# A third seven-product job in the input of a gated short convolution, and another order of the jobs around it

## The chip, the cores and the metric

The kernel runs on one core of a Trainium2 chip. The engines are TensorE (PE, with its weight loads PEld), VectorE (DVE), ScalarE (ACT), GpSimd (POOL) and SyncE (SP), which only issues DMAs. The metric is device microseconds of one execution, the median of three runs.

## The reference

The model has two layers on 512 tokens of width 1024, batch 1, float32: a gated short convolution with a SwiGLU, then sliding-window attention with a SwiGLU. The change lies in the first mixer alone:

```python
def short_conv_mixer(h, w_in, conv_w, w_out):
    bcx = h @ w_in
    b_gate, c_gate, u = jnp.split(bcx, 3, axis=-1)
    y = b_gate * causal_depthwise_conv3(c_gate * u, conv_w)
    return y @ w_out
```

Its input is rmsnorm(x) with a gain, its output is normed and added to x. Each of b, c and u is a product of 512 x 1024 by 1024 x 1024.

## The kernel before

**Numbers in two parts.** Every float32 matrix that enters a matmul is split into a high part (`whi`, a copy by ScalarE, in `split_weights` and `Job.prepare`, L500) and a low part (`wlo`, a subtraction on VectorE, L501). A product is three matmuls, `mm3`, L208 to L210. The channels of b, c and u are cut in eight tiles of 128, numbered f = 0 to 7; a tile's product over eight blocks of the inner dimension is a *project* of 24 matmuls of 512 columns (`pcub` in the rows).

**Seven products.** For c and u of two neighbouring tiles the kernel forms a 2 x 2 block product with seven block products in place of eight (`cross_jobs`, L908): four raw blocks a11, a12, a21, a22 of weights, sums of them made by VectorE (`make_two`, `make_three`, `make_four`, L917), sums of the tokens made once for all (`SUMMED`), and seven jobs of 24 matmuls of 256 columns. They collect in three PSUM banks, X for the products 1, 6, 7, 4, Y for 2, Z for 5 and 3 (`gx`, `gy`, `gz`). `take` reads the banks out between: products 1, 6 by ScalarE into `st`, 5 by ScalarE into `u`, 2, 3, 7 by a VectorE addition, 4 by two VectorE products which give c times u for both tiles in `gr`. Product 4 goes on adding in bank X, so its first matmul may start only when the take of product 7 (L949, `st<-gx`) has read it. Behind product 4 come, tile by tile: the product with the row norms (L854), a scaled copy by ScalarE and two taps by VectorE (L863), the product with b (L869). Tiles 2 and 3 then make a pair for the output product (sums and splits, L613 to L624); tiles 4 to 7 are split alone into `yhi` and `ylo` (L873, L874).

**Before the change** this form serves tiles 2, 3 (jobs X1 to X7) and 4, 5 (Y1 to Y7). b of these tiles is a project (b2 to b5, `gate_job`) which ScalarE copies from PSUM to SBUF (`bry`, L904). Tiles 6 and 7 have three projects each (c6 u6 b6, c7 u7 b7, `conv_jobs`), and the product with b reads PSUM. The output product of tiles 0 to 3 is again seven jobs P1 to P7 of 12 matmuls of 512 columns (`px`, `py`, `pz`), whose results go to `mix` by ScalarE's copies (L670) or VectorE's additions (L672). The weights of the other half, w0 to w3, are jobs that prepare and run nothing.

**What sets the order.** The string `CONV` lists the jobs by hand, and `in_line` (L505) runs them: run job j, prepare the weights of job j + 3 (`LINE_LEAD`), fetch raw blocks as buffers come free (`N_RAW` = 7 raw, `N_W` = 4 split ones), then one deferred step of an earlier job. Each of the engines PE, DVE, ACT and POOL keeps that order. `begin` and `pace` start sums of later weights by GpSimd's DMAs behind some jobs. Behind the line comes `close`: the output product of tiles 4 to 7 with w0 to w3 (`pmix`), in whose first part the weights of the feed-forward (gu, L438 and L443) are split, and which reads the parts of tile 7 last.

## Time and profile before

| | before |
|---|---|
| median of 3 runs | 1009.86 us (1009.26 to 1010.09) |
| the profiled execution | 1009.68 us |
| its span, first to last instruction | 1007.8 us |
| granted TensorE clock, mean | 0.999 |
| PE, DVE, ACT, POOL busy | 999.5, 911.1, 609.3, 184.3 us |
| DMA | 246.61 MB, mean 245 GB/s |

A row of a timeline has the start and the length in us, engine, line, operation, output and inputs by the program's names, the shape, the count of instructions merged in the row, and, in brackets, idle time before it with what ended it. Starts on an engine lie closer than the lengths, since an instruction begins while the one before drains; a step's price in a full queue is the distance of starts. The ends of matmuls are modelled. The rows of the trace carry the line numbers of the kernel before.

### The profile page before, as it was taken

What the parts mean: (1) busy time and instruction counts of PE and PEld (TensorE: products, weight loads), DVE (VectorE), ACT (ScalarE), POOL (GpSimd) and SP (SyncE); (2) the same over time, 40 slices, a digit from 0 to 9 for tenths busy, and PEclk for the clock granted to TensorE, in tenths of its full rate; (3) what the DMA queues carried; (4) which work ended last, traced back from release to release, by engine and by line L of the source; (5) the groups of instructions that cost most, each with busy time, mean ns of one, the idle gap of its engine ahead of it and who ended that gap; (6) DMA issues with size and microseconds to landing.
All of it is one profiled execution on the core that took longest, in us unless ns stands there. A gap on an engine that the chain in (4) does not pass through costs nothing.

```text
span 1007.8 us, 16460 instructions
## 1 busy us (share of the span) xinstructions
PE 999.5 (99%) x6008; PEld 886.7 (88%) x6008; DVE 911.1 (90%) x1564; ACT 609.3 (60%) x1105; POOL 184.3 (18%) x250
## 2 busy tenths in 40 slices
PE   9999999999999999999999999999999999999997
PEld 8899888999889898998898888799998988989986
DVE  7898878899799999999888998988997999999996
ACT  7445545875655455566485788777666564545641
POOL 0211021212111011000122756321201010110001
PEclk9999999999999999999999999999999999999999
DMA  9895988669979699779504889967989587979742
GB/s 338 263 260 181 334 283 288 204 194 286 343 243 297 220 303 321 236 219 336 193 1 138 216 245 245 292 242 170 305 285 319 167 251 237 289 272 276 243 167 83
DMA packets 67873, 246.61 MB, mean 245 GB/s; under 512 B 8017, under 2 KB 8657, under 8 KB 56017
## 3 DMA queue, kind: packets, MB, share of 16 engines
q1 hardware_dynamic: 52624, 148.07, 39.4%
q0 software_dynamic: 14592, 96.48, 37.7%
q8 instruction: 47, 0.77, 0.3%
q10 hardware_dynamic: 576, 1.02, 0.3%
q14 instruction: 34, 0.27, 0.1%
HBM read 239.25 MB, written 102.76 MB: 339 GB/s over the span
## 4 chain that ended last, share of the span: by engine, by line
PE 97%; DVE 2%; ACT 1%; issue 0%; DVEq 0%
PE gx L1282 15%; PE gx L1285 8%; PE px L208 4%; PE px L209 4%; PE px L210 4%; PE pmix L210 3%; PE pmix L208 3%; PE pmix L209 3%; PE gz L1282 3%; PE pcub L208 2%; PE pcub L210 2%; PE pcub L209 2%; PE gy L209 2%; PE gy L208 2%; PE gy L210 2%; PE pz L210 2%
## 5 line engine op out<-in xcount | busy, mean ns | idle before, releaser
L501 DVE TENSOR_TENSOR wlo<-raw,whi 128x1024 fp32r<-128x1024 f32 (+1 forms) x231 | 279.0, 1212 | 25.7 <-ACT whi L500 25.6
L500 ACT ACTIVATE whi<-raw 128x1024 fp32r<-128x1024 f32 (+1 forms) x231 | 239.7, 1051 | 79.2 <-DVE raw L488 37.7
L1282 PE MATMUL gx<-xt,whi 128*128 128x512 f32 x480 | 120.6, 393 | 0.0
L1282 PEld LDWEIGHTS gx<-xt,whi 128*128 128x128 f32 x480 | 86.2, 189 | 15.7
L571 POOL DMA_DIRECT2D hsum<-in_w_gb_dram x96 | 63.6, 727 | 163.0 <-ACT whi L500 107.8
L571 POOL DMA_DIRECT2D hsum<-hsum x32 | 25.2, 788 | 351.3 <-ACT whi L500 248.9
L1260 ACT ACTIVATE st<-gx 128x256 f32<-128x256 f32 x120 | 43.4, 380 | 60.9 <-PE gx L1285 57.3
L1237 DVE TENSOR_TENSOR st<-gx,st 128x256 f32<-128x256 f32 x200 | 77.4, 417 | 2.2 <-ACT st L1260 0.4
L1285 PEld LDWEIGHTS gx<-xt,wlo 128*128 128x128 f32 x480 | 65.5, 190 | 4.7
L1285 PE MATMUL gx<-xt,wlo 128*128 128x256 f32 x480 | 66.9, 282 | 0.0
L1296 ACT ACTIVATE gr<-gr 128x1024 f32<-128x1024 f32 x20 | 21.2, 1062 | 55.7 <-DVE gr L1237 55.7
L208 PE MATMUL gy<-xlo,whi 128*128 128x256 f32 x176 | 49.8, 283 | 0.0
L209 PE MATMUL gy<-xhi,whi 128*128 128x256 f32 x176 | 49.8, 283 | 0.0
L210 PE MATMUL gy<-xhi,wlo 128*128 128x256 f32 x176 | 49.8, 283 | 0.0
L208 PE MATMUL px<-wlo,ahi 128*128 128x512 f32 x120 | 46.7, 389 | 0.0
L209 PE MATMUL px<-whi,ahi 128*128 128x512 f32 x120 | 46.7, 389 | 0.0
L210 PE MATMUL px<-whi,alo 128*128 128x512 f32 x120 | 46.7, 389 | 0.0
L571 POOL DMA_DIRECT2D hsum<-in_w_dn_dram x48 | 32.0, 762 | 69.3 <-ACT whi L500 47.4
L1282 PE MATMUL gx<-xhl,whi 128*128 128x512 f32 x160 | 39.9, 391 | 0.0
L672 DVE TENSOR_TENSOR mix<-mix,px 128x512 f32<-128x512 f32 x54 | 34.8, 680 | 2.1 <-PE px L210 2.1
L318 POOL TENSOR_TENSOR ur<-uv,mhalf 128x1 f32<-128x1 f32 x15 | 13.9, 927 | 113.0 <-DVE uv L313 112.9
L488 DVE TENSOR_TENSOR raw<-raw,raw 128x1024 f32<-128x1024 f32 x28 | 34.1, 1218 | 0.1
(359 smaller groups left out, 3052.3 us busy)
## 6 DMA issues: line engine op xcount, KB each, us to landing
hsum<-in_w_gb_dram POOLq DMA_DIRECT2D x96, 512.0 KB, 8.0
raw<-hsum SPq DMA_DIRECT2D x88, 512.0 KB, 7.9
raw<-in_w_gb_dram SPq DMA_DIRECT2D x60, 512.0 KB, 6.9
hsum<-in_w_dn_dram POOLq DMA_DIRECT2D x36, 512.0 KB, 8.1
raw<-in_w_dn_dram SPq DMA_DIRECT2D x32, 512.0 KB, 7.0
hsum<-hsum POOLq DMA_DIRECT2D x28, 512.0 KB, 5.5
hsum<-in_w_dn_dram POOLq DMA_DIRECT2D x12, 768.0 KB, 13.5
raw<-in_w_in_dram SPq DMA_DIRECT2D x13, 512.0 KB, 7.2
```

The costliest lines, as they stand in the source:

```text
L208: nc.tensor.matmul(out, whi, xlo, start=start, stop=False, **kw)
L209: nc.tensor.matmul(out, whi, xhi, start=False, stop=False, **kw)
L210: nc.tensor.matmul(out, wlo, xhi, start=False, stop=stop, **kw)
L488: nc.vector.tensor_tensor(out=raw, in0=raw, in1=self.raws[1].tile, op=ALU.add)
L500: self.begun = nc.scalar.activation(hi[:, :n], raw, AF.Copy)
L501: nc.vector.tensor_tensor(out=lo[:, :n], in0=raw, in1=hi[:, :n].bitcast(F32), op=ALU.subtract)
L571: nc.gpsimd.dma_start(dst, src, max_dma_last_dim=4 * 4 * S, **kw))
L672: nc.vector.tensor_tensor(out=m, in0=m, in1=banks[bs][r], op=ALU.subtract if half else ALU.add)
L1237: nc.vector.tensor_tensor(out=out, in0=a, in1=b, op=ALU.add)
L1260: nc.scalar.activation(ste, a, AF.Copy)
L1282: nc.tensor.matmul(banks[c][e], whi[:, kk], factors[p][k][2], start=opened and k == 0, stop=False, **kw)
L1285: nc.tensor.matmul(banks[c][e][:, :256], wlo[:, kk], factors[p][k][0], start=False, stop=k == 3 and p in (4, 5), **kw)
```

## The change

`CROSS` goes from (2, 6) to (2, 8): c and u of tiles 6 and 7 become a third job of seven block products, Z1 to Z7, and c6, u6, c7, u7 go, with the function `conv_jobs`. The gates are spread: b4 stays between X and Y, b5 moves from behind Y6 to behind Y4, b6 stands between P6 and P3, b7 behind P4, w0 and w1. Where a tile's other factor is done before its gate (`later_on`: tiles 5, 6, 7), the product with b reads PSUM and ScalarE's copy falls away. The loads of x for the closing update (`hs`) are issued at the end of Z instead of Y. Their starts of sums move with the gates.

```diff
 CONV = (
-    "b2 b3 X1 X2 X6 X5 X7 X3 X4 b4 Y1 Y2 Y6 b5 Y5 Y7 Y3 Y4 c6 P1 P5 P6 P3 u6 P7 P2 P4 b6 w0 c7 u7 w1 b7 w2 w3"
+    "b2 b3 X1 X2 X6 X5 X7 X3 X4 b4 Y1 Y2 Y6 Y5 Y7 Y3 Y4 b5 Z1 Z2 Z6 Z5 Z7 Z3 Z4 "
+    "P1 P5 P6 b6 P3 P7 P2 P4 w0 w1 b7 w2 w3"
 )
-CROSS = (2, 6)
+CROSS = (2, 8)
...
-    BEGUN = {"X": {3: "c3"}, "Y": {6: "c4", 3: "c5"}}
+    BEGUN = {"X": {3: "c3"}, "Y": {6: "c4", 3: "c5"}, "Z": {}}
+    later_on = {}
     def gate_job(f, pool):
+        banks = []
         def products(job):
             ps = bank("pcub", pool)
+            banks.append(ps)
             project(ps, job.w, xs)
-            brs[f] = slot("bry")
-            nc.scalar.activation(brs[f], ps, AF.Copy)
-        return Job([Raw(w_in[f, 2])], products, begin("c2") if f == 3 else None)
+            if f not in later_on:
+                brs[f] = slot("bry")
+                nc.scalar.activation(brs[f], ps, AF.Copy)
+        def then():
+            parts = []
+            if f in later_on:
+                third, end = later_on[f]
+                parts = [lambda: third(banks[0])] + end()
+            if f in (3, 6, 7):
+                begin(f"c{f if f > 3 else 2}")()
+            if f < KT - 1:
+                return parts
+            for part in parts:
+                part()
+        return Job([Raw(w_in[f, 2])], products, then)
...
         def end():
-            steps = [conv(f + e, kept[2], brs.pop(f + e)) for e in range(2)]
-            parts = [lambda: [s[0]() for s in steps], steps[0][1], steps[1][1],
-                     lambda: [s[2](None) for s in steps]]
-            for s in steps:
-                parts += s[3]()
-            if f + 2 == CROSS[1]:
-                for b in range(NB):
-                    hs[b] = wide("h")
-                    tc.keep_in_program_order(nc.sync.dma_start(hs[b], x[b]))
+            steps = [conv(f + e, kept[2], brs.get(f + e)) for e in range(2)]
+            parts = [lambda: [s[0]() for s in steps], steps[0][1], steps[1][1]]
+            for e in range(2):
+                if f + e in brs:
+                    parts.append(lambda e=e: steps[e][2](None))
+                    parts += steps[e][3]()
+                else:
+                    later_on[f + e] = steps[e][2:]
+            if f < KT - 2:
+                return parts
+            for b in range(NB):
+                hs[b] = wide("h")
+                tc.keep_in_program_order(nc.sync.dma_start(hs[b], x[b]))
             return parts
-    def conv_jobs(f, pools):
...
-    for f, pool in zip(range(*CROSS), "ppmm"):
+    for f, pool in zip(range(*CROSS), "ppmmmm"):
         line[f"b{f}"] = gate_job(f, pools[pool])
-    for f, c in zip(range(*CROSS, 2), "XY"):
+    for f, c in zip(range(*CROSS, 2), "XYZ"):
         line.update(cross_jobs(f, c))
```

The order of instructions moves as follows; a number at a name is that of the buffer, and the lines of the kernel after stand one or some twenty higher.

VectorE in the Y block, from the sums of the pair of tiles 2 and 3 (`s`, `alo`) to the take of product 7 (`st<-gx`). Before, `wlo_1103` is Y3's low part and `wlo_1147` Y4's:

```order
L501 TENSOR_TENSOR wlo_1103<-raw_776,whi_1102 128x1024
L617 TENSOR_TENSOR s_929<-yy_926 128x256
L618 SCALAR_TENSOR_TENSOR s_929<-s_928,yy_926 128x256
L624 TENSOR_TENSOR alo_1117<-s_928,ahi_1116 128x512
L501 TENSOR_TENSOR wlo_1147<-raw_781,whi_1146 128x1024
L624 TENSOR_TENSOR alo_1155<-s_929,ahi_1154 128x512
L624 TENSOR_TENSOR alo_1159<-yy_926,ahi_1158 128x512
L949 TENSOR_TENSOR st_968<-gx_970,st_968 128x512
```

The same place after, with `wlo_1062` for Y3, `wlo_1109` for Y4 and `wlo_1146` for b5:

```order
L936 TENSOR_TENSOR raw_776<-raw_776,raw_579 128x1024
L870 TENSOR_TENSOR yy_926<-t_927,bry_666 128x512
L502 TENSOR_TENSOR wlo_1062<-raw_776,whi_1061 128x1024
L615 TENSOR_TENSOR a_231_930<-yy_926,a_231_930 128x256
L618 TENSOR_TENSOR s_928<-yy_926 128x256
L619 SCALAR_TENSOR_TENSOR s_928<-s_928,yy_926 128x256
L502 TENSOR_TENSOR wlo_1109<-raw_781,whi_1108 128x1024
L618 TENSOR_TENSOR s_929<-yy_926 128x256
L619 SCALAR_TENSOR_TENSOR s_929<-s_928,yy_926 128x256
L625 TENSOR_TENSOR alo_1117<-s_928,ahi_1116 128x512
L968 TENSOR_TENSOR st_968<-gx_970,st_968 128x512
L502 TENSOR_TENSOR wlo_1146<-raw_819,whi_1145 128x1024
```

The second product with b (`yy<-t,bry`) now stands between the sum of blocks and Y3's split, and the take stands two `alo` earlier. On TensorE the 24 matmuls of b5 no longer lie between Y6 and Y5.

ScalarE behind P4, whose bank goes to `mix` in two copies. Before, `raw_1427` is c7's block and `raw_1429` u7's:

```order
L192 ACTIVATE whi_1478<-raw_1191 128x512
L192 ACTIVATE whi_1479<-raw_1191 128x512
L670 ACTIVATE mix_1342<-px_1303 128x512
L670 ACTIVATE mix_1344<-px_1304 128x512
L500 ACTIVATE whi_1500<-raw_1427 128x1024
L500 ACTIVATE whi_1529<-raw_1429 128x1024
```

After, `raw_1630` is b7's block, and `raw_1632` and `raw_1760` are those of w2 and of the first gu:

```order
L193 ACTIVATE whi_1679<-raw_1399 128x512
L193 ACTIVATE whi_1680<-raw_1399 128x512
L276 DMA G_1687<-in_behind_dram 128x1024
L671 ACTIVATE mix_1546<-px_1508 128x512
L671 ACTIVATE mix_1548<-px_1509 128x512
L501 ACTIVATE whi_1704<-raw_1630 128x1024
L193 ACTIVATE whi_1708<-raw_1632 128x512
L439 ACTIVATE whi_1777<-raw_1760 128x1024
```

The two copies are followed by b7's high part where c7's stood, and the load of G comes ahead of them.

TensorE at the same place, after: the last matmuls of P4 and the first of b7 (before, the 24 of b6 follow P4):

```order
L209 MATMUL px_1509<-wlo_1627,ahi_1155 128x512
L210 MATMUL px_1509<-whi_1626,ahi_1155 128x512
L211 MATMUL px_1509<-whi_1626,alo_1156 128x512
L209 MATMUL pcub_1724<-xhl_221,whi_1704 128x512
L210 MATMUL pcub_1724<-xhl_221,whi_1704 128x512
L211 MATMUL pcub_1724<-xhl_221,wlo_1705 128x512
```

b7's first matmul stands right behind P4's last, and its third reads the low part.

More of the change, by code (lines that the diff above doesn't have):

```diff
@@ L1049, in yoco_kernel @@
     pools = {"p": ps_pt, "m": ps_mm, "s": ps_sc}
-    for f, pool in zip(range(*CROSS), "ppmm"):
+    for f, pool in zip(range(*CROSS), "ppmmmm"):
         line[f"b{f}"] = gate_job(f, pools[pool])
-    for f, c in zip(range(*CROSS, 2), "XY"):
+    for f, c in zip(range(*CROSS, 2), "XYZ"):
         line.update(cross_jobs(f, c))
-    for f, of in zip(range(CROSS[1], KT), ("mms", "spm")):
-        for c, job in zip("cub", conv_jobs(f, [pools[p] for p in of])):
-            line[f"{c}{f}"] = job
     for n in range(4):
```

28 lines of the change are left out of this document (removed).

## The prediction

> **What bounds the kernel now.** I read the page first (busy times and the chain that ended last), then who waits on TensorE over the whole span, then the window of the convolution input, then the order of time on TensorE, VectorE (DVE) and ScalarE (ACT) at the places that the change touches. The head of the page and of its chain:
>
> ```profile
> span 1007.8 us, 16460 instructions
> ...
> PE 999.5 (99%) x6008; PEld 886.7 (88%) x6008; DVE 911.1 (90%) x1564; ACT 609.3 (60%) x1105; POOL 184.3 (18%) x250
> ...
> PE 97%; DVE 2%; ACT 1%; issue 0%; DVEq 0%
> ```
>
> The waits of TensorE in the whole span (engine and line, whom it waited for, total us, times, longest), and the window that holds the stage (busy us and count of PE, PEld, DVE, ACT, POOL, then the granted clock, DMA share, GB/s):
>
> ```profile
> PE idle L748 <- DVE ones L152: 1.1, 1, 1.1
> PE pt L1603 <- DVE plo L1620: 0.4, 1, 0.4
> ```
>
> ```profile
> 46.00:153.00 107.00, 107.00 (x632) 95.47 (x631) 94.00 (x119) 52.65 (x74) 14.91 (x22) 1.00 0.85 262
> ```
>
> TensorE waits 1.5 us in all, and nowhere in this stage: it is the bound, and each microsecond of wait that the change makes lengthens the kernel, as each one of matmuls that it saves shortens it. VectorE comes second: 94.0 of 107.0 us, 13 us free.
>
> **What a matmul costs here.** Starts on TensorE, in order: first matmul of X4, of Y1, of b5 (behind Y1, Y2, Y6), of b6, and of the closing stage (behind b6, c7, u7, b7):
>
> ```profile
> 67.00 0.28 PE L208 MATMUL gx<-xf,whi 128*128 128x256 f32 x1
> ...
> 75.34 0.28 PE L208 MATMUL gx<-xhl,whi 128*128 128x256 f32 x1
> ...
> 83.98 0.40 PE L208 MATMUL pcub<-xhl,whi 128*128 128x512 f32 x1
> ...
> 130.90 0.39 PE L208 MATMUL pcub<-xhl,whi 128*128 128x512 f32 x1
> ...
> 152.66 0.39 PE L208 MATMUL pmix<-wlo,yhi 128*128 128x512 f32 x1
> ```
>
> Three jobs of 24 matmuls of 256 columns take 83.98 - 75.34 = 8.64 us, so 0.120 each and 2.88 a job. Four of 24 of 512 columns take 152.66 - 130.90 = 21.76, so 0.2267 each and 5.44 a job. The change takes c6, u6, c7, u7 out (96 matmuls, 21.76 us) and puts Z1 to Z7 in (7 x 2.88 = 20.16): **-1.60 us**, the whole of the gain, and under 0.2% (2.02 us), which is about what a measurement of this kernel tells from no change.
>
> [...] The rows above show 120 and 227, and the sum goes by them.
>
> **VectorE and ScalarE.** These rows of VectorE (start, length) price its steps by the distance from start to start. First those of the X block, then the beginning of the Y block:
>
> ```profile
> 56.53 0.68 DVE L869 TENSOR_TENSOR yy<-cut,pcub 128x512 f32<-128x512 f32 x1
> ...
> 57.73 1.22 DVE L501 TENSOR_TENSOR wlo<-raw,whi 128x1024 fp32r<-128x1024 f32 x1
> 58.86 1.22 DVE L917 TENSOR_TENSOR raw<-raw,raw 128x1024 f32<-128x1024 f32 x1
> 59.99 0.42 DVE L614 TENSOR_TENSOR a<-yy,a 128x256 fp32r<-128x256 f32 x1
> ...
> 61.21 1.23 DVE L501 TENSOR_TENSOR wlo<-raw,whi 128x1024 fp32r<-128x1024 f32 x1
> 62.35 0.42 DVE L617 TENSOR_TENSOR s<-yy 128x256 f32<-128x256 f32 x1
> ...
> 63.02 0.68 DVE L624 TENSOR_TENSOR alo<-s,ahi 128x512 fp32r<-128x512 f32 x1
> 63.62 1.22 DVE L501 TENSOR_TENSOR wlo<-raw,whi 128x1024 fp32r<-128x1024 f32 x1
> ...
> 65.96 0.68 DVE L949 TENSOR_TENSOR st<-gx,st 128x512 f32<-128x512 f32 x1
> ...
> 77.12 1.23 DVE L501 TENSOR_TENSOR wlo<-raw,whi 128x1024 fp32r<-128x1024 f32 x1 [1.75 <-ACT whi L500]
> 78.26 1.29 DVE L854 TENSOR_TENSOR gr<-gr,rrow 128x512 f32<-128x512 f32 x2
> ...
> 81.19 1.22 DVE L501 TENSOR_TENSOR wlo<-raw,whi 128x1024 fp32r<-128x1024 f32 x1
> 82.33 1.53 DVE L863 SCALAR_TENSOR_TENSOR t<-gr,gt,t 128x511 f32<-128x511 f32 x2
> 83.78 0.68 DVE L945 TENSOR_TENSOR gr<-gy,st 128x512 f32<-128x512 f32 x1
> ```
>
> A split of weights or a sum of blocks takes 1.13, a step on 512 columns 0.60, a pair of taps 1.45. The change adds three splits, four sums and five takes (3.4 + 4.5 + 3.0) and drops two products with u and two first taps (about 2.2): 8.7 us more, on VectorE, in 1.6 us less. Of 13 us free some 3 remain: enough in the mean, so what counts is where work piles up. ScalarE gets three splits more and loses copies; at 52.65 of 107 us its load costs nothing, its order does (below). DMA traffic stays the same, four blocks for four tiles of weights. The products with b read PSUM instead of a copy: as the first row above (yy<-cut,pcub, 0.68) shows, at the price of a product from SBUF. b5's bank is held some 17 us longer; its pool has four, and the next to want it is b6, 11 us after it is free.
>
> **Place 1: Y4.** In both orders the take of product 7 (st<-gx) reads the X bank that product 4 adds to, so Y4's first matmul waits for it. In the X block, where no gate stands between the seven, the take ended at 65.96 + 0.68 = 66.64 and X4 began at 67.00: 0.36 us to spare. Before, b5 stood in the Y block and gave VectorE 5.44 us more; now it comes behind Y4. Up to 82.33 nothing on VectorE moves (the row at 81.19 was b5's split and is now Y5's). From there its order is: taps to 83.78, third product and take of Y2 1.20 to 84.98, split of Y7 to 86.11, sum of blocks to 87.24 and third product to 87.84. Y3's split must wait for ScalarE, which can begin only when the sum has ended (86.11 + 1.22 = 87.33) and takes as long as here:
>
> ```profile
> 60.11 1.06 ACT L500 ACTIVATE whi<-raw 128x1024 fp32r<-128x1024 f32 x1 [0.91 <-DVE raw L917]
> ```
>
> So Y3's split runs from 88.45 to 89.59; three sums of the pair (59.99 to 61.21, 1.22) to 90.81; split of Y4 1.14 to 91.95; two sums 0.67 to 92.62; alo 0.60 to 93.22; the take ends 0.68 later, at 93.90. TensorE comes to Y4 at 75.34 + 6 x 2.88 = 92.62. **+1.3 us**; without the wait for ScalarE (0.6) and the pair's gap it would be 0.6, with a second wait of that size 1.9.
>
> **Place 2: Z4**, the same shape without pair sums. With Y4 from 93.92, TensorE comes to Z4 at 93.92 + 2.88 + 5.44 + 17.28 = 119.52. VectorE from 93.82: split of b5, two alo, take 3, split of Z1, sum, two takes, split of Z2, two sums (1.14 + 1.2 + 0.6 + 1.13 + 1.13 + 1.2 + 1.13 + 2.27 = 9.8) to 103.6; a wait of 1.2 for ScalarE's part of Z6; split, two products with the row norms, split of Z5, four taps, take 2, split of Z7, sum, third product (1.14 + 1.2 + 1.14 + 2.9 + 0.6 + 1.14 + 1.13 + 0.6 = 9.85) to 114.7; a wait of 0.6 for ScalarE's part of Z3; then split, ylo, split of Z4 with 0.2 of wait, third product of b5 and the take (1.14 + 0.6 + 0.2 + 1.13 + 0.6 + 0.68) to about 119.65. **+0.15 us**, between 0 and 0.5.
>
> **Place 3: b7.** A job's weights are split right behind the run of the job three places ahead in the line. Before, P4 was followed by b6 w0 c7: c7's split stood behind P4, and b6 ran meanwhile. Now it is P4 w0 w1 b7, and w0 and w1 run nothing on TensorE: b7's split stands behind P4 with no matmul between. On ScalarE it is queued behind the two copies of P4's bank, which wait for P4's last matmuls, and w2's and the next stage's splits queue behind it. c7's place in the trace:
>
> ```profile
> 130.42 1.28 ACT L670 ACTIVATE mix<-px 128x512 f32<-128x512 f32 x2 [4.55 <-PE px L210]
> 131.60 2.00 ACT L500 ACTIVATE whi<-raw 128x1024 fp32r<-128x1024 f32 x2
> ```
>
> P4 ended where b6 began, at 130.90, so the split starts 0.70 behind P4, its high part is ready at 0.70 + 1.05 = 1.75, VectorE's low part 1.22 + 0.03 later at 3.00, and with it the third matmul, the first that reads it. Without a wait that one starts at 2 x 0.2267 = 0.45. 2.55, and a little for TensorE to start again: **+2.6 us**, between 2.4 and 3.1 (before, VectorE came to that split 0.4 late). b7's raw block is no limit: by VectorE's steps the buffer that b6's split frees is its own, some 17 us ahead.
>
> **The end of the stage** I cost at nothing: y7's parts stand behind the splits of four weights of the feed-forward (gu), as before, when they ended 0.3 us ahead of the matmul that reads them:
>
> ```profile
> 154.05 0.68 DVE L869 TENSOR_TENSOR bry<-cut,pcub 128x512 f32<-128x512 f32 x1
> ...
> 155.78 0.68 DVE L874 TENSOR_TENSOR ylo<-bry,yhi 128x512 fp32r<-128x512 f32 x1
> ```
>
> The four loads of h move behind w1's on SyncE's queue, to about 119 us by VectorE's steps, and are first read in the closing stage's update.
>
> **Sum** on the profiled execution (1009.68, its span 1007.8 and 1.9 around it; 0.18 under the median of 1009.86): -1.60 + 1.3 + 0.15 + 2.6 = +2.45, so 1012.1, and by the median **1012.3 us**.
>
> **Rivals.**
>
> *VectorE keeps up* (not slower by the bound). Places 1 and 2 cost nothing, if the take of Y7 ends by 92.62, that is if VectorE does those steps 1.3 us faster than the X block's rows price them. For it: X4 had its 0.36 us to spare. Against: the Y block has 1.45 + 1.20 of taps and row norms more behind its second split. Time: -1.60 + 2.6 = +1.0, 1010.9. Should place 3 be covered too, 1008.3; the order speaks against that.
>
> *The gu weights come late.* Before, their buffers came free early. The first load was issued 14 us ahead of b7's first matmul, the fourth at 136.67, and they took (KB, median us to landing; the first load, then the fourth):
>
> ```profile
> 133.20 0.33 SPq L172 DMA_DIRECT2D raw<-in_w_gu_dram  x1
> ```
>
> ```profile
> raw<-in_w_gu_dram SPq DMA_DIRECT2D x1, 512.0 KB, 3.4
> ```
>
> ```profile
> raw<-in_w_gu_dram SPq DMA_DIRECT2D x1, 512.0 KB, 15.4
> ```
>
> Now they wait for VectorE's sum and split of P4, w0 and w1, by its prices from about 139.4 to 148. P4 ends at 119.67 + 2.88 + 7 x 12 x 0.2267 + 5.44 = 147.0, b7 at 147.0 + 2.6 + 5.44 = 155.1, y7 is read 18 matmuls later, at 159.2. The fourth load must land 1.06 + 1.22 + 0.68 (its splits and ylo) before that, by 156.2. At 4 us a load in a row it does (155.4). At the distance of before, (136.67 + 15.4 - 133.20 - 3.4) / 3 = 5.2, it lands at 160.2, 4.0 late. The middle, 2 us: 1014.3.
>
> *The clock falls.* [...] Here the clock (third last figure) is still whole 4 us behind the last matmul's start:
>
> ```profile
> 1000.84 0.28 PE L210 MATMUL pmix<-whi,alo 128*128 128x256 f32 x1
> ```
>
> ```profile
> 1004.00:1005.00 1.00, 0.00 (x0) 0.00 (x0) 0.64 (x1) 0.00 (x0) 0.00 (x0) 1.00 0.14 53
> 1005.00:1006.00 1.00, 0.00 (x0) 0.00 (x0) 0.00 (x0) 0.00 (x0) 0.00 (x0) 0.94 0.99 381
> 1006.00:1007.80 1.80, 0.00 (x0) 0.00 (x0) 0.00 (x0) 0.00 (x0) 0.00 (x0) 0.50 0.13 50
> ```
>
> b7's gap of 1.8 us is shorter. Were it to fall for 4 to 5 us, half of that would be lost, 2.2: 1014.5.
>
> **How the numbers follow.** Forecast 0.43, VectorE keeps up 0.21, all covered 0.04, gu late 0.30, clock 0.02. The forecast lies 0.4 us above the bound of +2.02, so I give 0.06 of its 0.43 to no change. Slower 0.37 + 0.30 + 0.02 = 0.69; the same 0.06 + 0.21 + 0.02 = 0.29; faster 0.02, half of all covered, since 1.6 us passes the bound only with scatter. The range runs from the first rival, 1010.9, to gu late with half a microsecond of the upper ends of places 1 and 3, 1014.8.
>
> **What would show it.** In the profile after: TensorE's waits list gx for VectorE's st at Y4 (about 1.3), at Z4 almost nothing, pcub for ScalarE's whi and VectorE's wlo at b7 (about 2.6), and nothing at pmix. Z's jobs take 2.88 each. No wait at Y4 means that VectorE keeps up; a wait of pmix for y7's parts means the gu loads; a wait under 2 us at b7 would make place 3 wrong.

## The result

| | before | after |
|---|---|---|
| median | 1009.98 us of 8 runs | 1014.66 us of 8 runs |
| lowest to highest | 1009.26 to 1010.38 | 1012.64 to 1020.91 |
| ratio, 95% interval | | 1.0064 [1.0047, 1.0081] |
| the profiled execution | 1009.68 (span 1007.8) | 1020.91 (span 1019.1) |

By the medians it is slower by 4.7 us; the forecast was 2.45. The median lies just inside the range (1010.9 to 1014.8), and three of the eight runs lie far above it. Sorted, the eight are 1012.64, 1014.01, 1014.65, 1014.66, 1014.66, 1019.95, 1020.16, 1020.91. By the means, 1016.46 and 1009.93, it is slower by 6.5 us, which is above the range; the ratio in the table is close to that of the means. Before has nothing like this spread, and much of what follows is about it. The profiled execution is the slowest of the eight, so its trace shows what the upper group of times is made of. From here on the lines are those of the kernel after, one or some twenty higher than before.

**The head of the page and of its chain, after:**

```profile
span 1019.1 us, 16611 instructions
...
PE 1002.2 (98%) x6080; PEld 890.2 (87%) x6080; DVE 919.3 (90%) x1572; ACT 613.9 (60%) x1110; POOL 184.3 (18%) x250
...
PE 88%; DVE 7%; ACT 2%; DMA 2%; issue 1%; DVEq 0%; ACTq 0%; SPq 0%
```

The chain was 97% TensorE; now 12% of it runs through the other engines and the DMAs. Whom TensorE waits for (total us, times, longest), where before there were two short waits, both outside of this stage:

```profile
PE pmix L209 <- ACT yhi L874: 3.9, 1, 3.9
PE pcub L209 <- ACT whi L501: 1.6, 1, 1.6
PE gx L209 <- DVE st L968: 1.2, 1, 1.2
...
PE pmix L209 <- DVE wlo L199: 1.0, 1, 1.0
PE pcub L211 <- DVE wlo L502: 0.5, 1, 0.5
```

`gx` is Y4 and `pcub` b7, both forecast. The `pmix` lines, which belong to the output products at the end of the stage, were to be absent: `yhi` is the high part of y7, and `wlo L199` the low part of a weight of the output product. Those matmuls in TensorE's order of time, with the first output product, the first one that reads y7, and the first matmul of the next stage (`xt`; before, 173.07):

```profile
94.01 0.36 PE L209 MATMUL gx<-xf,whi 128*128 128x256 f32 x1 [1.19 <-DVE st L968]
...
149.43 0.50 PE L209 MATMUL pcub<-xhl,whi 128*128 128x512 f32 x1 [1.63 <-ACT whi L501]
...
150.69 0.50 PE L211 MATMUL pcub<-xhl,wlo 128*128 128x512 f32 x1 [0.53 <-DVE wlo L502]
...
155.83 0.39 PE L209 MATMUL pmix<-wlo,yhi 128*128 128x512 f32 x1
...
165.27 0.80 PE L209 MATMUL pmix<-wlo,yhi 128*128 128x512 f32 x1 [3.92 <-ACT yhi L874]
...
184.32 0.93 PE L357 MATMUL xt<-ident,xn 128*128 128x128 f32 x7
```

This row of before closes the account:

```profile
173.07 1.14 PE L356 MATMUL xt<-ident,xn 128*128 128x128 f32 x9
```

The first output product comes 155.83 - 152.66 = 3.17 us later than before, the next stage 184.32 - 173.07 = 11.25 later, which is the whole difference of the two profiled executions (11.23). So 3.17 arose up to there and 8.08 in the 20 us behind it, where I had put nothing.

Behind it, ScalarE's order shows why. The four splits of gu stand ahead of y7's high part, and three of them wait for their loads (the `wlo` of the list is late for the same reason: its high part runs at 159.00, behind the third of them):

```profile
149.97 1.06 ACT L439 ACTIVATE whi<-raw 128x1024 fp32r<-128x1024 f32 x1
...
153.66 1.06 ACT L439 ACTIVATE whi<-raw 128x1024 fp32r<-128x1024 f32 x1 [2.10 <-DMA raw<-in_w_gu_dram]
...
158.03 1.06 ACT L439 ACTIVATE whi<-raw 128x1024 fp32r<-128x1024 f32 x1 [3.31 <-DMA raw<-in_w_gu_dram]
...
163.64 1.06 ACT L439 ACTIVATE whi<-raw 128x1024 fp32r<-128x1024 f32 x1 [3.52 <-DMA raw<-in_w_gu_dram]
164.61 0.61 ACT L874 ACTIVATE yhi<-bry 128x512 fp32r<-128x512 f32 x1
```

The loads are issued late, the first of the four at 140.12 (before, 133.20) and the last here (before, 136.67), which is 15.0 us on its way (KB, us to landing):

```profile
148.52 0.33 SPq L173 DMA_DIRECT2D raw<-in_w_gu_dram  x1
```

```profile
raw<-in_w_gu_dram SPq DMA_DIRECT2D x1, 512.0 KB, 15.0
```

Before, the last took 15.4, so it is not longer on its way; it starts 12 us later. SyncE waits for VectorE ahead of these loads, since their buffers come free by VectorE's splits and sums. Its waits at this line from 100 to 160 us, before and then after:

```profile
SPq L172 <- DVE wlo L198: 4.8, 2, 4.0
SPq L172 <- DVE wlo L501: 2.8, 3, 1.3
SPq L172 <- DVE wlo L443: 0.7, 1, 0.7
```

```profile
SPq L173 <- DVE wlo L199: 5.2, 2, 2.6
SPq L173 <- DVE wlo L502: 3.7, 2, 2.0
SPq L173 <- DVE raw L489: 3.4, 1, 3.4
```

It waited for VectorE before, too, 8.3 us in all; after, with 1.3 for `wlo L444`, it is 13.6.

And while TensorE stands for y7, the clock (third last figure) goes to half:

```profile
163.00:164.00 1.00, 0.00 (x0) 0.00 (x0) 0.00 (x0) 0.36 (x1) 0.00 (x0) 0.71 1.26 336
...
165.00:170.00 5.00, 4.61 (x10) 3.21 (x11) 3.53 (x5) 1.43 (x4) 0.00 (x0) 0.50 1.00 413
...
170.00:171.00 1.00, 1.00 (x5) 0.77 (x5) 0.75 (x3) 0.23 (x2) 0.38 (x1) 0.88 1.03 422
```

Those shares put it at half from about 163.4 to 170.2, 6.8 us. Of these TensorE had work in the last 4.9 and lost about half of it, 2.45 at most. The stands (3.92 + 1.00) and this make up to 7.4 of the 8.08; the rest I did not follow.

### The profile page after: what moved, and what is told of

It reads as the page before. It is cut to its first block, busy times and chain, and to the rows that moved or that the text cites. A ratio compares the mean times of both kernels' runs of the same rounds, so it can differ in the third digit from the quotient of the medians.

```text
span 1019.1 us, 16611 instructions
## 1 busy us (share of the span) xinstructions
PE 1002.2 (98%) x6080; PEld 890.2 (87%) x6080; DVE 919.3 (90%) x1572; ACT 613.9 (60%) x1110; POOL 184.3 (18%) x250
## 4 chain that ended last, share of the span: by engine, by line
PE 88%; DVE 7%; ACT 2%; DMA 2%; issue 1%; DVEq 0%; ACTq 0%; SPq 0%
PE gx L1269 14%; PE gx L1272 7%; PE px L209 3%; PE px L210 3%; PE px L211 3%; PE pmix L211 3%; PE pmix L209 3%; PE pmix L210 3%; PE gz L1269 3%; PE gy L210 2%; PE gy L209 2%; PE gy L211 2%; PE pcub L785 2%; PE pz L211 2%; PE pz L210 2%; PE pz L209 2%
## 5 line engine op out<-in xcount | busy, mean ns | idle before, releaser
L502 DVE TENSOR_TENSOR wlo<-raw,whi 128x1024 fp32r<-128x1024 f32 x234 | 282.7, 1212 | 26.2 <-ACT whi L501 25.9
L501 ACT ACTIVATE whi<-raw 128x1024 fp32r<-128x1024 f32 x234 | 243.0, 1051 | 88.8 <-DVE raw L489 34.9
L209 PE MATMUL gy<-xlo,whi 128*128 128x256 f32 x184 | 52.1, 283 | 0.0
L210 PE MATMUL gy<-xhi,whi 128*128 128x256 f32 x184 | 52.1, 283 | 0.0
L211 PE MATMUL gy<-xhi,wlo 128*128 128x256 f32 x184 | 52.1, 283 | 0.0
L209 PEld LDWEIGHTS gy<-xlo,whi 128*128 128x128 f32 x184 | 35.3, 192 | 0.0
```

The source lines that it names most:

```text
L209: nc.tensor.matmul(out, whi, xlo, start=start, stop=False, **kw)
L210: nc.tensor.matmul(out, whi, xhi, start=False, stop=False, **kw)
L211: nc.tensor.matmul(out, wlo, xhi, start=False, stop=stop, **kw)
L501: self.begun = nc.scalar.activation(hi[:, :n], raw, AF.Copy)
L502: nc.vector.tensor_tensor(out=lo[:, :n], in0=raw, in1=hi[:, :n].bitcast(F32), op=ALU.subtract)
```

## The experiments

A stand is a stretch in which TensorE has nothing that it may run. The theory with which I went in: the stands at Y4 and b7 set 3 us, and late gu loads the rest. Rivals: one of the three alone carries it; the clock does; VectorE's load does. Ratios are to the kernel before in the same session, with the 95% interval.

### The kernel after once more

**e1**, unaltered.

> The changed kernel once more, unaltered, for the spread of its times and a second profile. Theory (the four gate and up loads land when other transfers let them, 11 to 15 us after their issue, and the clock falls or stays by how long TensorE then stands): times again in separate groups near 1012.6, 1014.5 and 1020 us, and in a profile of a run at 1012 to 1015 us the wait of the first output tile's last part for y of tile 7 is 1 to 3 us instead of 3.9, with the clock whole through 160 to 172 us. Rival (a fixed cost somewhere else, and one disturbed profile): the same 3.9 us wait in every profile, whatever the time, and the clock at half beside it.

1014.58, 1014.66, 1015.65, 1018.16, 1022.45, 1022.74: 1.0082 [1.0057, 1.0107]. The profiled execution is one of 1014.66. It has no wait at `pmix`, since its fourth load came in 9.6 us and was split at 158.47, but its clock fell behind b7's stand:

```profile
150.00:151.00 1.00, 0.47 (x3) 0.06 (x1) 1.00 (x2) 1.00 (x2) 1.00 (x2) 0.96 0.86 283
151.00:152.00 1.00, 1.00 (x3) 0.81 (x4) 1.00 (x2) 0.62 (x2) 0.58 (x1) 0.50 0.99 402
154.00:155.00 1.00, 1.00 (x5) 0.78 (x5) 1.00 (x1) 0.91 (x1) 0.00 (x0) 0.83 0.88 205
```

Half from about 150.9 to 154.3, 3.4 us. Its output products begin and its next stage starts here:

```profile
157.63 0.39 PE L209 MATMUL pmix<-wlo,yhi 128*128 128x512 f32 x1
...
178.03 1.14 PE L357 MATMUL xt<-ident,xn 128*128 128x128 f32 x9
```

That is 1.80 later than in the profile above, and 4.97 later than before; from there to the next stage it takes 20.40, as before (20.41). In such an execution nothing is lost at the end of the stage. Of the 1.8 beyond the three places (Y4, Z4 and b7), 0.26 arose earlier (b7's first matmul starts at 149.69 instead of 149.43), and 1.5 is the clock.

### One place at a time, then all

**e2**, b5 back into the Y block.

```diff
-... Y6 Y5 Y7 Y3 Y4 b5 Z1 ...
+... Y6 b5 Y5 Y7 Y3 Y4 Z1 ...
```

> One job moved: the product for b of tile 5 goes back behind Y6, so product 7 of Y has a job to read while VectorE empties the bank that Y4 waits for; the rest is as in the changed kernel. Theory: the 1.2 us wait at Y4 goes and nothing else does, so 1.2 us under the changed kernel's times, about 1013.2 us for the most frequent kind, with the b7 wait of 1.6 and the wait for y of tile 7 still there. Rival 1 (the wait moves: VectorE falls behind by another 0.7 us and Z4 or P waits as long instead): the same time as the changed kernel, 1014.5. Rival 2 (the order of loads shifts and with it the gate and up landings): a change of 2 us or more either way, with the landings moved in its profile.

1.0050 [1.0038, 1.0062], median 1014.62. The stand of 1.2 at Y4 is gone, and two of 0.5 have come, in the Z and P blocks:

```profile
PE gz L211 <- DVE wlo L502: 0.5, 1, 0.5
PE px L209 <- ACT whi L501: 0.5, 1, 0.5
```

b6 begins at 131.25, in the kernel after at 131.31. Y4's wait was VectorE's arrears; they are paid further on.

**e3**, y7's parts free to go ahead of the gu splits (the closing stage's order no longer fixed by hand).

```diff
-    opening.close()
...
-    with tc.manual_schedule(engines=ALL):
-        close(ws, ys, 0, res, ahead)
+    close(ws, ys, 0, res, ahead)
+    opening.close()
```

> The order of jobs of the changed kernel, but the input line and the output products stand in one list, so that on ScalarE and VectorE the last output splits and the two parts of y of tile 7 come ahead of the four splits of gate and up weights, which wait for their loads. Theory (the lost time at the end of the stage is those parts standing behind splits that wait for loads, and the fall of the clock follows from that standstill): the waits of 1.0 and 3.9 us in the output products go to under 0.5 together, the clock stays whole from 120 to 200 us, no time near 1020, and the median is 1009.98 - 1.60 + 1.27 + 0.1 + 2.6 = about 1012.3 us, within 0.7. Rival 1 (the clock falls by the sum of small stops at 147 to 152 us, whatever comes behind): half the clock at about 163 us still, and times near 1015 and up. Rival 2 (the splits are only late elsewhere: the first feed-forward products wait for gate and up weights instead): about the same time as the changed kernel, 1014.5, with a wait of 2 us or more in front of the first gate products.

1.0044 [1.0031, 1.0057], median 1014.28 (expected, 1012.3), one run of 1018.22, which is the profiled one. TensorE no longer stands for y7. In its place the first norm waits, behind the same fourth split, which the same load holds back:

```profile
PE xt L357 <- ACT xn L346: 3.7, 1, 3.7
```

```profile
163.59 1.06 ACT L439 ACTIVATE whi<-raw 128x1024 fp32r<-128x1024 f32 x1 [3.47 <-DMA raw<-in_w_gu_dram]
```

**e4**, e2, e3 and b7 ahead of P4, so that P4 runs while b7's weights are split (the diff shows what comes to those of e2 and e3).

```diff
-P2 P4 w0 w1 b7 w2 w3
+P2 b7 P4 w0 w1 w2 w3
```

> All three repairs: b of tile 5 back behind Y6, b of tile 7 ahead of P4 (so that its split does not queue behind P4's copies with no product in between), and y of tile 7 ahead of the gate and up splits. Theory (the three places together are all of the loss, and the 1.60 us of matmuls saved are real): 1009.98 - 1.60 = 1008.4 us, to 1009.0 with small waits left at Z4, faster than both kernels. Rival (the saved matmuls are taken up by later work, since something off TensorE, VectorE at 90 % of the span, sets the end of the stage): 1009.9 us and above, with new waits of 1.5 us or more between 115 and 175 us.

1.0096 [1.0082, 1.0109], median 1019.4. The stands at Y4, b7 and y7 are all gone, the first output product comes at 153.49, 2.3 us earlier than after, and the kernel is no faster for it: its four runs lie at 1019.15 to 1019.7, while e1's in the same session spread from 1014.58 to 1022.74 around 1016.9. Expected were 1008.4 to 1009.0. TensorE's waits now:

```profile
PE pmix L209 <- DVE mix L280: 5.0, 1, 5.0
PE xt L357 <- ACT xn L346: 1.8, 1, 1.8
```

ScalarE awaits the loads of the last two gu splits for 4.6 and 2.7 us, and what TensorE waits for comes behind them. VectorE shows it for the first wait, the low part of the fourth split and the take behind it:

```profile
167.83 1.23 DVE L444 TENSOR_TENSOR wlo<-raw,whi 128x1024 fp32r<-128x1024 f32 x1 [2.48 <-ACT whi L439]
168.97 1.28 DVE L280 TENSOR_TENSOR mix<-pmix,mix 128x512 f32<-128x512 f32 x2
```

This refutes "the waits are prices that can be added up". What ends last here is a chain beside TensorE: buffer, load, split.

### The splits out of the way

**e5**, e3 with the third and fourth gu splits behind the second and third of the takes that read out the output products (L280). **e6**, e5 with nine filler matmuls in b7's bank, whose result is overwritten. **e8**, "Y3 b5 Y4", "P2 b7 P4", e3's free order, the two splits in the second output tile (its diff is against e5), and the sums of e7 (below).

```diff
-            for _ in range(each if half == 0 or each > 1 else 0):
+            for _ in range(1 if late else each if half == 0 or each > 1 else 0):
...
+                if late and (t, half) in ((0, 1), (1, 0)):
+                    ahead.one()
```

```diff
+            for _ in range(9 if f == KT - 1 else 0):
+                nc.tensor.matmul(ps, ones_r, xs[0][0], start=True, stop=True)
             project(ps, job.w, xs)
```

```diff
-                if late and (t, half) in ((0, 1), (1, 0)):
+                if late and t == 1:
                     ahead.one()
```

> The order of jobs of the changed kernel. The input line and the output products stand in one list, as in the run where y of tile 7 went first, and beside that the third and fourth split of the gate and up weights are emitted behind the takes of the first output tile and of the first half of the second, so that nothing of the norms stands behind a load that comes late. Theory (two things beyond the three places cost the time: parts that queue on ScalarE and VectorE behind splits whose loads land late, and half a clock for about 3.4 us behind a standstill; the second happens in some executions only): no wait of TensorE over 0.6 us between 152 and 190 us, times of two kinds, 1009.98 - 1.60 + 1.2 + 0.2 + 2.4 = 1012.2 us with the clock whole, and 1.7 us more, 1013.9 us, where it falls behind the standstill at b7; none over 1014.7. Rival (what is queued behind does not matter, the transfers themselves take longer, and the standstill only moves on, to the first gate products): times of 1016 us and over again, with a wait of 2 us or more after 176 us.

> The kernel with the late splits, and nine further products of 512 columns into b7's own bank, whose result is overwritten, ahead of b7's products: TensorE works through the 2.15 us in which it stood there. The further products compute nothing that is kept. Theory (the clock falls because TensorE stands; the stand is 1.6 us and 0.5 us more): the nine products take 9 x 0.227 = 2.04 us, so the end comes no later, the clock stays whole in 148 to 156 us, and all times are of the one kind, 1012.2 us (1011.8 to 1012.8). Rival (the clock falls for another reason, such as the many transfers in that stretch or a fixed moment of the execution): half the clock in 151 to 154 us also here and two kinds of times as in the kernel without the nine.

> All repairs together: b of tile 5 between Y3 and Y4, b of tile 7 ahead of P4, one list, the third and fourth split of gate and up weights behind the second output tile's takes, and the five sums issued at about 189 us. Theory (no standstill is left, so the clock stays whole, and the 1.60 us of matmuls saved come through): 1009.9 - 1.6 = 1008.3 us, up to 1009.0 with waits of 0.5 us at Z1 and P1. Rival (VectorE, busy for all but 0.1 us of 120 to 140 us, has no room: what is saved on TensorE is waited for in other places): 1009.7 to 1011 us, with waits of 1 us and more for VectorE between 90 and 180 us.

e5 1.0090 [1.0075, 1.0105], e6 1.0092 [1.0077, 1.0107], e8 1.0115 [1.0100, 1.0130]. All miss what was expected. In e5 and e6 the norm waits 4.2 us. In e8 the first output product comes at 152.52, as early as before (152.66), with no stand at Y4, b7 or y7: some 1.4 of the 1.6 us that the matmuls save is spent in small stands in Z and P. Its median is 1021.4:

```profile
PE xt L357 <- ACT xn L346: 5.0, 2, 4.7
PE px L209 <- DVE mix L673: 1.8, 1, 1.8
```

The first line is the norms (`xt`): the third and fourth split now run in the second output tile, with their low parts on VectorE, among the norms' own steps. The second stands at 295 us, where e7 stands too, and belongs to the sums that e8 takes over from e7; so e8 is no clean test of the order alone. Filling b7's stand (e6) changes nothing while the norms come last.

### The traffic beside the loads

Five moving sums of later weights (`sum_on("c7")`, `sum_on("o0")`), DMAs from GpSimd's queue, start beside the last gu loads. After, GpSimd's issues:

```profile
149.67 0.82 POOL L572 DMA_DIRECT2D hsum<-hsum  x1 [11.09 <-ACT whi L501]
...
152.87 1.81 POOL L572 DMA_DIRECT2D hsum<-in_w_gb_dram  x3 [1.54 <-DMA hsum<-in_w_gb_dram]
```

**e7** starts them at about 189 us, **e10** between the norms of the first output tiles, some 16 us later than after; **e14** is e10 again.

```diff
-            if f in (3, 6, 7):
+            if f in (3, 6):
                 begin(f"c{f if f > 3 else 2}")()
...
-    sum_on("o0")
-    issue(len(issues))
...
-                        sum_on("o1")
+                        for at in ("c7", "o0", "o1"):
+                            sum_on(at)
```

```diff
-    def close(ws, x, k0, res, ahead, each=2, sooner=False):
+    def close(ws, x, k0, res, ahead, each=2, sooner=False, sums=()):
...
+                if t < len(sums):
+                    sum_on(sums[t])
+                    issue(len(issues))
...
-        close(ws, ys, 0, res, ahead)
+        close(ws, ys, 0, res, ahead, sums=["c7", "o0"])
```

(e10 has the first two pieces of e7's diff and this.)

> The changed kernel with five of the moving sums taken out of 149 to 155 us and issued behind the norms at about 189 us; nothing else is changed, and the gate and up splits stand where the change has them, ahead of y of tile 7. Theory (the third and fourth load of gate and up weights land late because five sums of 0.5 to 0.75 MB go out beside them): the fourth lands by 157 us in every execution, the wait for y of tile 7 is under 0.5 us, and the times are of the two kinds 1012.6 and 1014.6 us (the second with half a clock behind b7), none over 1015.7. Rival (the loads land late because they are issued late, up to 148.5 us, whatever goes beside them): waits of 1 to 4 us for y of tile 7 in the profile and times of 1016 us and over in a fifth of the runs or more.

> As the kernel with the quiet loads, but the five moving sums are issued between the norms of the first output tiles, about 16 us later than in the changed kernel instead of 40, so that the sums which the first down products read are not late at 272 and 295 us. Theory (with the sums out of the way the gate and up weights land in time, and nothing else is worth more than 0.5 us): fourth load landed by 157.5 us, no wait over 0.5 us for y of tile 7 and none at 270 to 300 us, times of two kinds, 1012.6 to 1013.1 us and, where the clock falls behind b7, 1014.2 to 1014.9; none over 1015.7. Rival (the sums have no 16 us to give, or they block the norms on GpSimd): waits of TensorE over 1 us at 170 to 190 or at 270 to 300 us and times of 1015 us and over.

> The kernel with the sums between the norms a second time, unaltered: in its first group all five times lay at 1012.9 to 1014.0 us and the clock stayed whole behind the stand at b7, where in three other kernels with the same stand it fell. Theory (with the sums away no load is waited for; whether the clock falls behind b7 is chance of the single execution): no time over 1015.7 us again, and times of both kinds, 1012.9 to 1013.4 and 1014.2 to 1014.9. Rival (the few late sums left or the loads themselves are late in some executions also here): times of 1016 us and over.

e7 1.0091 [1.0074, 1.0108]: no wait for y7, but the sums are themselves wanted at 272 to 295 us, and TensorE stands there (1.4 and 3.3), so that e7 alone proves nothing for the time. e10 1.0034 [1.0021, 1.0047], median 1013.2; e14 1.0037 [1.0024, 1.0049], median 1013.34. The fourth gu load as e14's trace has it (KB, us to landing; 15.0 after), and what follows on TensorE:

```profile
raw<-in_w_gu_dram SPq DMA_DIRECT2D x1, 512.0 KB, 6.5
```

```profile
155.82 0.39 PE L209 MATMUL pmix<-wlo,yhi 128*128 128x512 f32 x1
...
176.24 0.93 PE L357 MATMUL xt<-ident,xn 128*128 128x128 f32 x7
```

3.16 later than before at the first output product, 3.17 at the next stage: in this execution, 1012.92, the three places are all that is left. In e10's, 1014.03, another 1.0 us goes behind the first output product (the next stage begins at 177.31): its second load landed 1.1 us later, and y7's parts with it. Of the 15 runs of e10, e14 and e15 none lies above 1014.6. Of the 36 of after, e1, e2, e3, e9 and e13, where the sums are as they were, 13 are at 1016 or more; e2 has none of them, e3 one. The traces say the same of the fourth load. Without these sums beside it, it took 6.5 us in e14 and 7.5 in e10, with them 9.6 in e1 and 15.0 in after. Its split starts by 157.5 in six traces without them (e7, e10, e11, e12, e14, e15); with them it waits 2.3 to 3.5 us for the load and starts at 158.47 to 166.75 in six (after, e1, e3, e4, e9, e13), but at 157.3 in e2.

### The clock at b7

**e9**, seven fillers in a spare bank ahead of b7. **e15**, the same on e10.

```diff
+            if f == KT - 1:
+                fill = bank("fill", pool)
+                for _ in range(7):
+                    nc.tensor.matmul(fill, ones_r, xs[0][0], start=True, stop=True)
```

> The changed kernel with seven further products of 512 columns into a spare bank ahead of b7's products, where TensorE stood for 1.6 us and then 0.5 us; they compute nothing that is kept. The scheduler then also places four output products among b7's first ones. Splits, loads and sums stay where the change has them. Theory (the half clock at 151 to 154 us comes from that stand; where it does not come, y of tile 7 is ready about 1.6 us earlier and the fourth gate and up load, if it lands after 157 us, is waited for instead): clock 1.00 in 148 to 156 us of the profile, seven products take 1.6 us of the stand, so the first output product comes 1.5 to 2 us earlier than in the changed kernel's second profile (157.63); times near 1012.6 us where the fourth load lands by 157 us, 1016 to 1020 where it lands later, and none at 1014.0 to 1015.7. Rival (the clock falls whatever TensorE does there): 0.6 to 0.7 of the clock in 150 to 155 us again and most times at 1014.6 us.

> The same with seven further products of 512 columns into a spare bank ahead of b7's (not kept), so that TensorE hardly stands there; the scheduler then places four output products among b7's first. Theory (a stand of 2.15 us is what the clock falls behind; without it and without late loads one kind of time is left): 1012.3 to 1013.2 us in all runs, none over 1013.8, the clock whole from 20 to 200 us. Rival (the clock falls by chance, stand or no stand): times of 1014 us and over here as often as in the kernel without the seven.

e9 1.0068 [1.0044, 1.0092], median 1015.66. In its profiled execution, 1014.87, the clock is whole throughout, and TensorE waits 2.0 us for y7:

```profile
PE pmix L209 <- ACT yhi L874: 1.4, 1, 1.4
...
PE pmix L211 <- DVE ylo L875: 0.6, 1, 0.6
```

None was expected at 1014.0 to 1015.7. So a time near 1014.7 is reached in two ways: the clock falls at b7, TensorE comes 1.8 us later to y7 and finds it ready (e1), or the clock holds and TensorE waits for y7 (e9). In these two executions they do not add. e15 1.0037 [1.0023, 1.0051], median 1013.41, beside e14 in one session at 1013.34: no gain. The fillers take up the 1.63 us in which TensorE would have stood; behind them four output products slip in ahead of b7's third matmul, and b7 ends a little later. VectorE's product with b7 starts at 158.03 instead of 157.74 (e14), and the next stage begins at 176.52 instead of 176.24. One run of e15 takes 1014.49, where none over 1013.8 was expected; its mean clock is whole (0.999), so the clock is not all of the upper kind of times. Two of e14's, 1014.33 and 1014.51, have a mean clock of 0.996.

### VectorE, and the best version

**e11**, e10 with "Y3 b5 Y4" and one filler in b7's bank, which lets nine output products go into b7's stand. **e12**, e11 with the low parts of gu on GpSimd (the helper is given the engine). **e13**, the kernel after without the taps of tiles 6 and 7 on VectorE.

```diff
-... Y7 Y3 Y4 b5 Z1 ...
+... Y7 Y3 b5 Y4 Z1 ...
...
+            if f == KT - 1:
+                nc.tensor.matmul(ps, ones_r, xs[0][0], start=True, stop=True)
             project(ps, job.w, xs)
```

```diff
-                ahead.one()
+                ahead.one(nc.gpsimd if sums else nc.vector)
```

```diff
-            for lag, tap in ((1, 1), (2, 0)):
+            for lag, tap in ((1, 1), (2, 0)) if f < KT - 2 else ():
```

> b of tile 5 between Y3 and Y4; one further product (0.23 us, not kept) in b7's bank, by which the scheduler places the nine first output products, 2.04 us, ahead of b7's products, where TensorE stood; the sums between the norms. Theory: 1009.86 + 3.18 (what the changed kernel loses up to its output products, with the clock whole) - 1.35 (Y4) - 2.76 (b7) + 0.23 + 0.5 to 1.5 (y of tile 7 is then waited for, since only nine products lie before its use) = 1009.7 to 1010.7 us, one kind of time, with the clock whole to the end of the output products. Rival (VectorE is the bound of this stretch, and each wait removed comes back elsewhere): 1012 us and above, with waits of 1 us or more in 100 to 150 us that the changed kernel does not have.

> The kernel with b5 between Y3 and Y4, the first output products ahead of b7's and the sums between the norms, in which the low halves of the four gate and up weights are now taken on GpSimd instead of VectorE: 4 x 1.22 = 4.9 us off VectorE between 150 and 160 us; on GpSimd they should take about 2.6 to 3.1 us each, by the 1.54 us of its 512-column ones. Theory (VectorE, which the change gave 8 us more work, is now what the end of the input stage waits for): y of tile 7 no longer queues behind the third and fourth low half, its two waits of 1.2 and 0.3 us go to under 0.4 together, the first transposes come 1.2 us earlier or more, and the median is 1010.2 to 1010.8 us instead of 1011.9. Rival (the stage is bound by the loads, or by b7's own chain, the engine of the low halves makes no difference): 1011.5 to 1012.2 us again; or later by a microsecond where the norms on GpSimd now queue behind the low halves.

> The changed kernel without the four taps of tiles 6 and 7 of the convolution (two multiply-adds of each left out, 4 x 0.75 = 3.0 us less on VectorE between 133 and 138 us); so part of the result is left out. The scheduler then also puts four output products among b7's first ones. Sums, loads and splits keep their order. Theory (the gate and up loads go out late because their buffers come free by VectorE's low halves, and VectorE is full): the four loads go out 2 to 3 us earlier than at 140.1, 142.5, 145.5 and 148.5 us, the last one at least 1 us earlier; the stand at b7, which hangs on ScalarE's queue behind P4's copies, stays 1.6 us; times then mostly of the kind of 1012.2 to 1013 us, or 1014 to 1014.6 with half a clock behind b7, and those of 1016 us and over in fewer than a fifth of the runs. Rival (the buffers come free by TensorE's pace, and VectorE's load only fills its idle time): the loads go out within 0.5 us of where they did, and the spread of times is that of the changed kernel.

e11 1.0023 [1.0014, 1.0031], median 1011.86 of 11 runs, the best found and still slower than before (expected, 1009.7 to 1010.7). The stands at Y4 and b7, 3.3 us, shrink to 0.2. The time is 1.3 below e10's, by as much as its first gu load goes out earlier (e10, then e11):

```profile
140.16 0.33 SPq L173 DMA_DIRECT2D raw<-in_w_gu_dram  x1
```

```profile
138.86 0.33 SPq L173 DMA_DIRECT2D raw<-in_w_gu_dram  x1
```

The rest of the 3.1 has become a wait for y7 (1.2) and stands in Z and P (0.5 the longest). This fits the chain of loads, but the version differs in two edits, so it is no proof of the 1.3.

e12 1.0070 [1.0058, 1.0082] does not answer its question, since three of VectorE's subtractions took 8.24 us in place of 2.04 while GpSimd subtracted (last section). e13 1.0053 [1.0036, 1.0071], median 1015.64: its loads go out at 139.30 to 147.91, 0.8 and 0.6 us earlier (expected, 2 to 3), and the spread is that of the kernel after. Four taps less on VectorE, 3 us, do not bring the loads back; the rest of its added work I did not take apart.

## Why the prediction was wrong

**Matmuls, Y4, b7: right.** The window from the Y block to b7, before and then after:

```profile
90.00:150.00 60.00, 60.00 (x310) 51.56 (x309) 49.46 (x63) 32.51 (x46) 6.66 (x11) 1.00 0.95 308
```

```profile
90.00:150.00 60.00, 57.05 (x350) 50.62 (x348) 56.22 (x71) 31.54 (x45) 6.27 (x11) 1.00 0.91 276
```

VectorE (third pair) is at 56.2 of 60; over the whole program it is busy 919.3 - 911.1 = 8.2 us more, where I had 8.7. Z's jobs take 2.88 each. Y4's first matmul was forecast at 93.92 and came at 94.01, 1.35 later than right behind Y3's last one (forecast 1.3). b7's stand was to have one part, and has two, of 1.63 and 0.53; with the slow first matmuls behind them it costs 155.83 - 5.44 - 147.64 = 2.75 (forecast 2.6), where 147.64 is the end of P4: 149.43 - 1.63, less 0.16 because a matmul's modelled end lies 0.39 behind its start and the next starts 0.23 behind it.

**Z4: too small.** P4's end was forecast at 147.0 and came at 147.64, with 0.09 of it from Y4. So Z and P have about 0.7 of small stands, where I had 0.15: Z4's first matmul, at 119.99, comes 0.29 late and holds up the next by 0.07, and a stand at 128.5 in P takes 0.2. The four terms make 3.2 instead of 2.45, as e14's trace has it; by their medians e10 and e14 measure +3.5 and +3.4. To this point the forecast holds within its range.

**What failed is "The end of the stage I cost at nothing".** I compared TensorE's new order with itself and let y7's parts stand "as before". But before, they had 0.7 us to spare (`ylo` ended at 156.46, the matmul that reads it starts at 157.20; my 0.3 went to the first matmul of y7, which reads `yhi`), and the change moves the loads ahead of them 7 to 12 us back on SyncE's queue. What the runs showed in place of nothing is 8.08 us in the profiled execution of after, 0 in e14's and 0 in e1's. I saw that the loads might come late, and put it as a rival of its own with 0.30 and 2 us. Its mechanism was right: buffers that VectorE frees late, loads from 140 to 148.5 (I had 139.4 to 148), a wait of `pmix` for y7's parts. Its size is no figure but a spread, since the fourth load takes 6.5 us without the moving sums beside it, and 9.6 or 15.0 with them (e14, e1, after). I had a fixed distance of loads, and no word of the sums. TensorE stands for nothing there or for up to 4.9 us, and in the latter case the clock comes down too. So of the 2.2 us by which the median passes the forecast, some 0.8 is the small stands, and about 1.5, what e10 wins back, belongs to this step and the next point; by the means it is 4.1 us, of which about 3 belong to them. That the median lies inside the range is partly luck: the three runs near 1020 do not move it.

**The clock: right to name, wrong to dismiss** (0.02). I reasoned that b7's 1.8 us is shorter than the 4 us at the end of the program that left it whole. In e1 it fell for 3.4 us behind stands of 1.63 and 0.53 with two matmuls between, and cost 1.5 of the 1.8 by which this execution passes the three places. The 4 to 5 us of half clock in the rival's price came from no row; the falls in the traces last 3.4 us or about 6.8 (last section). Of the eight profiled executions with b7's stand as after has it (after, e1, e2, e3, e5, e7, e10, e14), it fell there in three (e1, e2, e7); of the seven with no stand of 1 us at b7 (e4, e6, e8, e9, e11, e12, e15) in none, and e13, with the first of the two stands alone, kept the clock whole there.

**Joined, not apart.** I shared the chance out as if one of the rivals would come true. Two did, the late loads and the clock, beside the forecast itself, and they hang together: late loads make stands, and in the traces the clock falls in or behind stands: at b7 (1.63 and 0.53 us, in e1, e2 and e7), for y7 (3.9 in after, 2.9 in e12, 1.3 and 0.6 in e13), for a take (5.0, e4) or for the norm (3.7 to 4.7, in e3, e5, e6 and e8). What makes the loads go out late is argued, not shown. VectorE's added work may do it, or the order itself, in which P4, w0 and w1 now free the buffers; e13, with 3 us less on VectorE, moved them by only 0.6 to 0.8 us. "VectorE keeps up" was wrong, since `gx` waited 1.2.

**What stays open:** what decides in which execution the clock falls, why e2's fourth split could start at 157.3 with the sums beside its load, and whether VectorE's added work or the order makes the loads late. Loads from buffers of their own, which would take SyncE's wait away, were not tried.

## What to carry to other kernels

A wait on the bound engine (the one whose time sets the kernel's) is a price only if nothing else ends at the same time; of each change ask what is late next, and follow the buffers that a busier engine frees to the loads that wait for them. Where such a load ran beside bulk traffic its landing was a spread (9.6 and 15.0 us with the moving sums, 6.5 and 7.5 without), so give the forecast as one, and move the traffic before the order (here 1.5 us by the median and the whole upper group of times, while the removal of the stands at Y4, b7 and y7, in e4 and e8, gained nothing). Rivals that hang together come true together.

## What the runs showed of the hardware

**The clock's falls came in two lengths.** 3.4 us in e1; 6.8, twice that, after. From 147 to 190 us it falls in eleven of the traces, once in each, to 0.50 where a window lies whole inside the fall, and at that clock the shares put every fall at 3.4 us (e1, e2, e3, e4, e6, e7, e13) or about 6.8 (after, e5, e8, e12). Behind stands of 1.63 and 0.53 us at b7 it fell in three executions of eight. What sets the two lengths, and in which execution it falls, no trace here shows.

**VectorE beside GpSimd.** In e12 four subtractions on GpSimd and what VectorE did meanwhile, three subtractions that end to end are 0.68 each:

```profile
150.46 10.93 POOL L444 TENSOR_TENSOR wlo<-raw,whi 128x1024 fp32r<-128x1024 f32 x4 [12.87 <-ACT whi L439]
```

```profile
150.93 8.24 DVE L199 TENSOR_TENSOR wlo<-raw,whi 128x512 fp32r<-128x512 f32 x3 [0.16 <-ACT whi L193]
```

2.04 us of work took 8.24, about 2.7 each, as long as one of GpSimd's (10.93 / 4). It does not hold for all of VectorE's work in that stretch: its product with b7, which reads PSUM, took 0.68 at 159.10, as elsewhere. The low part of y7 took 1.47 at 160.47, where 0.68 is its length elsewhere. What makes the subtractions so long beside GpSimd's, the trace does not show.
